# A tiled 8192 x 8192 transpose: the first load issued as two halves from two engines, and the last wait moved to VectorE

## Chip, cores and metric

The kernel runs on one core of a Trainium2 chip. The metric is the time of one execution on the device, in microseconds. A profile of one execution lies beside the times. In it PE is TensorE, DVE is VectorE, ACT is ScalarE, POOL is GpSimd and SP is SyncE.

## What is computed

```python
x = np.random.randn(8192, 8192).astype(np.float32)

def reference(x):
    return np.transpose(x)
```

The matrix has 8192 x 8192 float32 elements, 268 MB. It is read once and its transpose is written once.

## The kernel before

The input is cut into 128 chunks of 128 rows by 4096 columns (2 MB each): `chunks` at line 99 runs over two column halves `s` and, within each, over 64 row blocks `c`. A chunk is loaded whole into one of three buffers, `in0` to `in2`, each with 128 partitions of 16 KB (`NIN` is 3, so chunk `t` goes to buffer `t % 3`).

TensorE transposes a chunk in 32 blocks of 128 x 128 against an identity matrix into PSUM (`transposes`, lines 112 to 123). Its program is a loop, `turns`, of three chunks a turn. ScalarE copies the first half of a chunk's blocks from PSUM to SBUF, VectorE the second half (line 241). The copies go into nine regions of one SBUF tensor, `regs`. Each region gathers the columns of up to eight chunks (`W` is 8), so that a store can write long runs; the eight windows are offset by one chunk against each other, so that about one of them closes per chunk. A region that is complete is stored by one DMA (line 174 the first, line 28 the rest) from ScalarE's queue. In the first eight chunks the closing windows are still short, and the stores grow from 256 KB to 2 MB; the last chunk closes all eight, and these eight stores stand at the end.

The order of the work around the change:

- GpSimd builds the identity matrix (lines 85 to 94).
- The loads of the first three chunks are issued from SyncE (`load`, line 103), one behind the other on its queue. In the code these three calls stand behind TensorE's loop. Every later load is issued from ScalarE, and stands in its program behind the copies and stores of the chunk that freed the buffer (lines 261 to 264).
- Each input buffer has one semaphore, `s_ld[k]`. TensorE starts on a chunk when it reaches 18 and takes 18 off (line 113): 16 come from the load's DMA, 1 each from ScalarE and VectorE, which increment it when they have copied the chunk that was there before and thereby free PSUM. For the very first chunk there is nothing to copy before, so lines 96 and 97 give the two increments at once.
- Each region has a semaphore `s_st[r]`, raised by 16 for each of its stores. At the end SyncE waits for all nine regions (lines 265 and 266), so that the kernel ends only when every store has landed. `free` is the list of regions in the order in which their stores were issued; its last entry is the region that was stored last.

Of the kernel before, what the change touches and what calls it, by code (L numbers as in the profile page):

```python
# [40 lines left out]
def kernel(  # L41
# [13 lines left out]
    nc = tc.nc  # L55
    P = 128
# [8 lines left out]
    NIN = 3  # L65
    NREG = 9
    CH = N // P
    J = S * P

    with tc.tile_critical():  # L70
        nc.alloc_sbuf_tensor("pad", [P, 32], dt)
        ident = nc.alloc_sbuf_tensor("ident", [P, P], dt).ap()
        ins = [nc.alloc_sbuf_tensor(f"in{k}", [P, J], dt).ap() for k in range(NIN)]
# [6 lines left out]
        s_ld = [nc.alloc_semaphore(f"s_ld{k}") for k in range(NIN)]  # L80
        s_st = [nc.alloc_semaphore(f"s_st{k}") for k in range(NREG)]
# [6 lines left out]
            out=ident,  # L88
            in_=ident,
# [3 lines left out]
            pattern=[[-1, P]],  # L93
            channel_multiplier=1,
        ).then_inc(s_id, 1)
        nc.vector.sem_inc(s_ld[0], 1)
        nc.scalar.sem_inc(s_ld[0], 1)

        chunks = [(s, c) for s in range(M // J) for c in range(CH)]

        def load(t):
            s, c = chunks[t]
            (nc.sync if t < NIN else nc.scalar).dma_start(
                out=ins[t % NIN], in_=x[c * P:(c + 1) * P, s * J:(s + 1) * J]
            ).then_inc(s_ld[t % NIN], 16)

        def transposes(k):
            nc.tensor.sem_inc(s_ld[k], -18).wait_op(s_ld[k], 18, "sem-ge")  # L113
            for q in range(NR):
                e, g = divmod(q, NH)
                for b in range(B):
                    tr = nc.tensor.transpose(  # L117
                        pss[e][:, (g * B + b) * P:(g * B + b + 1) * P],
                        ins[k][:, q * B * P + b:(q + 1) * B * P - B + b + 1:B],
                        ident,  # L120
                    )
                if q % 2:
                    tr.then_inc(s_pe, 1)
# [15 lines left out]
            nc.regs_alu(turn, turn, 1, op=mybir.AluOpType.add)  # L139
            nc.tensor.br_lt(turn, T // NIN + 1, on_true="turns", on_false="done")  # L140
        nc.switch_bb("done")

        for t in range(NIN):
            load(t)

        copied = [0, 0]
        free = list(range(NREG))
        stored = [0] * NREG
# [36 lines left out]
        for t, (s, c) in enumerate(chunks):  # L185
            closed = []
            for e in range(2):
# [5 lines left out]
                for q in range(e * NH, (e + 1) * NH):  # L193
                    if q not in window:
# [4 lines left out]
                        r = free.pop(0)  # L199
# [6 lines left out]
                    t0, r, parts = window[q]  # L206
# [54 lines left out]
            if t + NIN < T:  # L261
                if not closed:
                    nc.scalar.wait_ge(s_pe, (t + 1) * NH)
                load(t + NIN)
        for r in range(NREG):
            nc.sync.wait_ge(s_st[r], 16 * stored[r])


# [28 lines left out]
```

## Time and profile before

| | |
|---|---|
| time, median of 3 runs | 1261.94 us (1261.61 to 1261.95) |
| span of the profiled execution | 1260.4 us |
| TensorE matmul, busy | 739.0 us |
| VectorE, busy | 302.0 us |
| ScalarE, busy | 253.5 us |
| moved by DMA | 536.95 MB, mean 426 GB/s |
| DMA packets on SyncE's queue (q1) and ScalarE's (q10) | 432 and 38832 |

The span is the time from the first to the last instruction of the profiled execution; that execution is known by its span alone, and the times of the runs are longer than it by some 1.5 us. In a row of a timeline stand the start, the time taken, the engine ("SPq" and "ACTq" are the instruction queues of SyncE and ScalarE, where a DMA is issued), the line, the operation, and in brackets the idle time before it with what ended it. A row of a table by stretches holds the stretch, its length, the busy time of PE, of its weight loads, of DVE, ACT and POOL with the number of instructions, the granted TensorE clock, the busy share of the 16 DMA engines and their GB/s; a packet is booked where it starts, so that neighbouring short stretches can differ by more than the stream does. In a row of one source line stand the operation's count, its least, median and greatest duration in ns, and the starts of the first and the last.

### The profile page before, as it was taken

The page shows a single profiled execution, that of the slowest core. Times are in us where ns is not written, and L with a number is a line of the kernel's source. Part 1 is how long each engine was busy: PE and PEld are TensorE (multiplying, and loading weights), DVE is VectorE, ACT ScalarE, POOL GpSimd, SP SyncE. Part 2 cuts the span into 40 slices and gives each one's busy share as a digit, 9 for nine tenths or more (in the row PEclk, how much of TensorE's full clock was granted, in tenths as well). Part 3 has the DMA queues.
Part 4 walks back from the last instruction along what each step waited for, and adds up shares of the span by engine and source line. Part 5 has one row for each costly group of instructions (what it writes and reads, how often), then busy time and mean ns, then how long its engine had stood idle before and what let it go on. Part 6 is the DMA issues. An engine that isn't in the chain of part 4 may idle for free. (4 is left out here: it accounts for less than half of the span.)

```text
span 1260.4 us, 9367 instructions
## 1 busy us (share of the span) xinstructions
PE 739.0 (59%) x4096; PEld 718.4 (57%) x4096; DVE 302.0 (24%) x250; ACT 253.5 (20%) x257; POOL 0.7 (0%) x6
## 2 busy tenths in 40 slices
PE   5656556565566655565556656566565655665561
PEld 5556556565556655565555656565565655665561
DVE  2322222222222222222222222222222222222220
ACT  3212211122111211122111211121111211121110
POOL 0000000000000000000000000000000000000000
PEclk9886876868777777778687786867777687777776
DMA  9999999999999999999999999999999999999998
GB/s 383 429 422 426 425 430 431 426 431 431 427 430 431 428 428 431 428 429 432 427 422 426 429 429 425 431 429 428 430 428 428 431 428 429 429 429 429 429 431 376
DMA packets 39271, 536.95 MB, mean 426 GB/s; under 512 B 4320, under 2 KB 4832, under 8 KB 6240
## 3 DMA queue, kind: packets, MB, share of 16 engines
q10 hardware_dynamic: 38832, 530.60, 99.0%
q1 hardware_dynamic: 432, 6.29, 1.2%
q14 instruction: 6, 0.05, 0.0%
q8 instruction: 1, 0.02, 0.0%
HBM read 268.44 MB, written 268.44 MB: 426 GB/s over the span
## 5 line engine op out<-in xcount | busy, mean ns | idle before, releaser
L117 PE MATMUL ps<-ident,in 128*128 128x128 f32 x4096 | 739.0, 362 | 493.5 <-PEq L113 493.5
L117 PEld LDWEIGHTS ps<-ident,in 128*128 128x128 f32 x4096 | 718.4, 220 | 513.9 <-issue 513.9
L241 DVE COPY regs<-ps 128x512 f32<-128x512 f32 (+3 forms) x250 | 302.0, 1246 | 932.1 <-PE ps L117 932.1
L241 ACT COPY regs<-ps 128x512 f32<-128x512 f32 (+3 forms) x256 | 252.2, 1016 | 978.8 <-PE ps L117 760.8
L241 ACT ACT_TABLE_LOAD x1 | 1.3, 1283 | 1.0 <-SPq L70 1.0
L87 POOL TENSOR_SCALAR_AFFINE_SELECT ident<-ident 128x128 f32<-128x128 f32 x1 | 0.3, 293 | 0.2 <-POOL ident L85 0.2
L85 POOL MEMSET ident<- 128x128 f32 x1 | 0.2, 204 | 0.5 <-SPq L70 0.5
L281 POOL MEMSET const-bfloat16-1.0<- 128x1 bf16 x1 | 0.1, 102 | 0.0
L281 POOL MEMSET const-uint8-127<- 128x1 uint8 x1 | 0.1, 102 | 0.0
L281 POOL MEMSET const-float32-0.0<- 128x1 f32 x1 | 0.1, 99 | 0.2 <-issue 0.2
L281 POOL MEMSET const-float32-1.0<- 128x1 f32 x1 | 0.1, 99 | 0.0
## 6 DMA issues: line engine op xcount, KB each, us to landing
in<-in_x_dram ACTq DMA_DIRECT2D x125, 2048.0 KB, 16.8
out_dram<-regs ACTq DMA_DIRECT2D x114, 2048.0 KB, 12.6
out_dram<-regs ACTq DMA_DIRECT2D x4, 1792.0 KB, 11.1
in<-in_x_dram SPq DMA_DIRECT2D x3, 2048.0 KB, 11.7
out_dram<-regs ACTq DMA_DIRECT2D x4, 1536.0 KB, 12.5
out_dram<-regs ACTq DMA_DIRECT2D x4, 1280.0 KB, 11.5
out_dram<-regs ACTq DMA_DIRECT2D x4, 1024.0 KB, 11.1
out_dram<-regs ACTq DMA_DIRECT2D x4, 768.0 KB, 12.3
```

The lines of the kernel that those rows point to most:

```text
L85: nc.gpsimd.memset(ident, 0.0).then_inc(s_id, 1)
L87: nc.gpsimd.affine_select(out=ident, in_=ident, compare_op=mybir.AluOpType.not_equal, fill=1.0, base=0, pattern=[[-1, P]], channel_multipl ...
L117: tr = nc.tensor.transpose(pss[e][:, (g * B + b) * P:(g * B + b + 1) * P], ins[k][:, q * B * P + b:(q + 1) * B * P - B + b + 1:B], ident,)
L241: cp = nc.scalar.copy(out=o, in_=i) if e == 0 else nc.vector.tensor_copy(out=o, in_=i)
L281: nc = _bacc.Bacc("TRN2", target_bir_lowering=False, num_devices=1)
```

## The change

The first chunk's load becomes two DMAs. ScalarE issues partitions 0 to 63, SyncE partitions 64 to 127, both as the first DMA of their queue. ScalarE's half raises `s_ld[0]` by 16; SyncE's half raises a new semaphore, `s_l0`. ScalarE adds its 1 right after the issue. VectorE waits for `s_l0` and then adds its 1, so that the 18 are complete only when both halves are in. The three first loads now stand ahead of TensorE's loop in the code. At the end VectorE waits for the region that was stored last, and SyncE for the other eight.

```diff
-        nc.vector.sem_inc(s_ld[0], 1)
-        nc.scalar.sem_inc(s_ld[0], 1)
+        s_l0 = nc.alloc_semaphore("s_l0")
...
         def load(t):
             s, c = chunks[t]
-            (nc.sync if t < NIN else nc.scalar).dma_start(
-                out=ins[t % NIN], in_=x[c * P:(c + 1) * P, s * J:(s + 1) * J]
-            ).then_inc(s_ld[t % NIN], 16)
+            src = x[c * P:(c + 1) * P, s * J:(s + 1) * J]
+            if t == 0:
+                nc.scalar.dma_start(out=ins[t][:P // 2], in_=src[:P // 2]).then_inc(s_ld[t], 16)
+                nc.sync.dma_start(out=ins[t][P // 2:], in_=src[P // 2:]).then_inc(s_l0, 16)
+                nc.scalar.sem_inc(s_ld[t], 1)
+                nc.vector.wait_ge(s_l0, 16)
+                nc.vector.sem_inc(s_ld[t], 1)
+                return
+            (nc.sync if t < NIN else nc.scalar).dma_start(out=ins[t % NIN], in_=src).then_inc(s_ld[t % NIN], 16)
+
+        for t in range(NIN):
+            load(t)
...
         nc.switch_bb("done")
-
-        for t in range(NIN):
-            load(t)
...
         for r in range(NREG):
-            nc.sync.wait_ge(s_st[r], 16 * stored[r])
+            (nc.vector if r == free[-1] else nc.sync).wait_ge(s_st[r], 16 * stored[r])
```

## The prediction

> **What bounds the kernel now.** I read the page's head and DMA rows first, then the engines' busy shares and issue rows, then a table by stretches.
>
> ```profile
> span 1260.4 us, 9367 instructions
> PE 739.0 (59%) x4096; PEld 718.4 (57%) x4096; DVE 302.0 (24%) x250; ACT 253.5 (20%) x257; POOL 0.7 (0%) x6
> ...
> DMA  9999999999999999999999999999999999999998
> ...
> DMA packets 39271, 536.95 MB, mean 426 GB/s; under 512 B 4320, under 2 KB 4832, under 8 KB 6240
> q10 hardware_dynamic: 38832, 530.60, 99.0%
> q1 hardware_dynamic: 432, 6.29, 1.2%
> HBM read 268.44 MB, written 268.44 MB: 426 GB/s over the span
> ```
>
> No compute engine is busy for more than 59% of the span, while the 16 DMA engines are busy in every slice. Queue q10 (ScalarE's, 530.60 MB) carries nearly everything; q1 (SyncE's) carries 6.29 MB, the first three loads of 2.1 MB each. So the kernel is a stream of 536.95 MB, and its end is start of stream + bytes over rate + what follows the last byte. The table by stretches shows these pieces:
>
> ```profile
> 2.00:4.00 2.00, 0.00 (x0) 0.00 (x0) 0.00 (x0) 0.26 (x1) 0.00 (x0) 1.00 0.91 303
> 4.00:14.00 10.00, 5.50 (x32) 5.34 (x32) 1.03 (x2) 2.15 (x4) 0.00 (x0) 1.00 1.02 436
> 14.00:24.00 10.00, 6.70 (x53) 6.57 (x54) 3.94 (x7) 3.49 (x7) 0.00 (x0) 1.00 0.99 386
> 100.00:1230.00 1130.00, 677.45 (x3694) 658.94 (x3695) 271.14 (x214) 225.69 (x222) 0.00 (x0) 0.75 1.01 429
> ```
>
> The last two columns are the DMA engines' busy share and GB/s. The stream runs saturated: 436 GB/s over 4 to 14 us, when the first loads are alone in it, and 429 GB/s in the long middle. There is no idle DMA time between, so **a microsecond lost to the stream anywhere comes out at the end, and a microsecond won by another engine does not**, as long as the stream always has something queued. The chain of waits names PE and VectorE near the end, but VectorE's last copies end at 1234, and the rest is the drain of stores:
>
> ```profile
> 1231.57 2.48 DVE L241 COPY regs<-ps 128x512 f32<-128x512 f32 x4 [7.54 <-PE ps L117]
> ```
>
> **The start, and the cover in it.**
>
> ```profile
> 0.94 1.32 SPq L103 DMA_DIRECT2D in<-in_x_dram  x3
> 0.94 0.20 POOL L85 MEMSET ident<- 128x128 f32 x1 [0.50 <-SPq L70]
> 0.98 1.28 ACT L241 ACT_TABLE_LOAD   x1 [0.98 <-SPq L70]
> ...
> 8.40 5.50 PE L117 MATMUL ps<-ident,in 128*128 128x128 f32 x32 [8.40 <-PEq L113]
> ...
> 11.01 0.63 ACTq L174 DMA_DIRECT2D out_dram<-regs  x1
> ...
> 12.97 2.48 DVE L241 COPY regs<-ps 128x512 f32<-128x512 f32 x4 [12.97 <-PE ps L117]
> 13.94 0.36 ACTq L103 DMA_DIRECT2D in<-in_x_dram  x1
> ```
>
> ```profile
> 1.50:2.00 0.50, 0.00 (x0) 0.00 (x0) 0.00 (x0) 0.50 (x1) 0.17 (x1) 1.00 0.00 0
> 2.00:2.25 0.25, 0.00 (x0) 0.00 (x0) 0.00 (x0) 0.25 (x1) 0.00 (x0) 1.00 1.67 328
> ```
>
> ```profile
> 2.00:3.00 1.00, 0.00 (x0) 0.00 (x0) 0.00 (x0) 0.26 (x1) 0.00 (x0) 1.00 1.01 262
> ```
>
> ```profile
> L103 ACTq DMA_DIRECT2D in<-in_x_dram x125: 334/607/1218, 13.9 to 1210.1; - x125
> L103 SPq DMA_DIRECT2D in<-in_x_dram x3: 372/423/427, 0.9 to 1.8; - x3
> ...
> DMA to landing us min/median/max: 7.3/16.8/19.8
> ```
>
> The first data moves between 2.00 and 2.25. The first load is issued at 0.94 and lands 7.3 us later, at 8.2; PE begins at 8.4. Each further load takes 2.097 MB / 436 GB/s = 4.81 us, so the three are in at about 8.2 + 2 x 4.81 = 17.9. The fourth load is issued at 13.94, and its data can begin about 1.1 us after (the first issue at 0.94 gives data from about 2.0), at 15.0. Hence PE may begin up to 17.9 - 15.0 = **2.9 us later** before the stream runs dry. That is why an earlier PE start is worth nothing here.
>
> **The change part by part.**
>
> 1. *Loads written ahead of the PE loop.* SyncE's first issue stands at 0.94, the same moment as GpSimd's memset that already stood ahead of that loop. Both follow the same release. Nothing to win: 0.
>
> 2. *Two issues instead of one.* ScalarE issues its 64 rows where its semaphore increment stood (about 0.9), SyncE its 64 rows at 0.94, then loads 1 and 2. An issue of 128 rows costs SyncE 372 to 427 ns. If half the rows cost half, data may start up to 0.2 us earlier; if not, nothing is won. I take -0.1. ScalarE pays one more issue (334 to 1218 ns by its own rows) and its 1.28 us table load moves behind it or stays ahead of it. Its next work is the copy at 10.4, so at most 2.5 us lie beside about 8 us of waiting. If the table load stays ahead, ScalarE's half starts 1.28 us late; PE would then be late by that, inside the cover of 2.9 us.
>
> 3. *How fast two halves travel.* This is the term that decides. No row of this trace shows a load of 64 rows; all have 128 rows, and there 436 GB/s belongs to 16 DMA engines and 128 partitions at once. If the rate belongs to the engines, two halves on two queues move as the whole did, 4.81 us: cost 0, or slightly below with item 2. If it belongs to the partitions being written (3.4 GB/s a row), a half alone goes at 218 GB/s. Then it matters whether all engines work on the same half at a time. A 16 KB row of a load takes an engine 16384 B / (436/16 GB/s) = 0.60 us, and the stretch of 2 to 3 us moved 262 KB, which is 16 such rows: all engines start within less than two rows' time. Engines that start so close together and take rows from two queues in turn all serve the same half for much of the time, and stay so, since the turns are equally long. Fully in step, the first 2.1 MB take 9.62 us instead of 4.81: **+4.81** is the upper end. The nearest row with two queues in the stream is 14 to 24 us (the first store, issued at 11.01, beside the third load, which ends near 18): 386 GB/s at a busy share of 0.99, against 436 at 1.02. Engines just as busy moved 11% less, which on the first load would be 4.81 x 436/386 - 4.81 = +0.6; but small store pieces are in that row, so it prices only a mild case. I take three quarters of the upper end, **+3.6**, because engines partly out of step lose less, and because the slowest engine, not the average, sets when a load has landed and when the stream ends. Both ends, 0 and +4.8, are kept for the range.
>
>    [...]
>
>    The loss is not hidden: PE starts at about 12 instead of 8.4 and the fourth load is issued 3.6 us later, but the first three loads end 3.6 us later too, so the cover of 2.9 us stays as it was, nothing runs dry, and the whole later stream is shifted by 3.6.
>
> 4. *VectorE waits for SyncE's half and then increments.* Queued behind that wait are only its increment and its first copy, at 12.97, which waits for PE anyway. PE waits for the increment: one more semaphore hop, about 0.1 us by the distance between the first landing (8.2) and PE's wait and start (8.3, 8.4). It lies in the 2.9 us cover: 0. Without cover, 0.1.
>
> 5. *The last wait on VectorE.*
>
> ```profile
> L266 SPq EVENT_SEMAPHORE  x4: 27/28/4912, 1250.4 to 1254.3; - x4
> ```
>
> ```profile
> L70 SPq EVENT_SEMAPHORE  x3: 17/28/28, 1259.4 to 1259.6; - x3
> L70 SPq NOP  x2: 13/13/13, 0.7 to 1259.7; - x2
> L70 SPq COMPARE_BRANCH  x1: 33/33/33, 1259.2 to 1259.2; - x1
> ...
> L70 DVEq DRAIN  x1: 17/17/17, 1259.4 to 1259.4; - x1
> ```
>
>    SyncE's last wait starts at 1254.3 and lasts 4.9 us, to 1259.2. Then come its branch (1259.2), its signal (1259.4), the other engines' drains (1259.4), and the closing barrier to 1260.4. If VectorE waits instead, SyncE's signal and three of the drains are done early, and only VectorE's wake, branch and drain follow the last landing. VectorE was done with its copies at 1234, so nothing is queued behind it. At best that saves the step from the wait's end to the signal, 0.2 us; at worst VectorE's branch and drain take as long, 0. I take -0.1.
>
> Sum: 1260.4 + 0 - 0.1 + 3.6 + 0 - 0.1 = 1263.8. The span before is 1260.4, the median of the three times 1261.94, so 1.5 us lie around the span: **1265.3 us**, +3.4 or 0.27%.
>
> **The rivals.**
>
> - *The halves run at full rate (the other side: not slower).* The rate belongs to the engines, or the two halves keep out of step so that all 128 partitions are served at once. For it: in every long row the busy share is about 1.0 whatever mix of loads and stores runs, so the engines look like the limit. Against it: such a row never has fewer than 128 partitions in any one transfer. Then only items 2 and 5 count: 1261.94 - 0.2 = 1261.7, and between 1261.3 and 1262.0. The point from which it decides: the first load lands by 8.5 or earlier.
> - *Partly in step.* Some engine pairs collide, others don't, or the loss is of the kind in the 14-to-24 row: +0.6 to +2.4, so about 1263.3.
> - *The stream runs dry.* ScalarE's half comes late (table load ahead, a slow issue up to 1.2 us): 1.28 + 1.2 = 2.5 us of delay to PE against 2.9 us of cover. At full rate it costs nothing; it would decide only above 2.9 us. I count it within the first rival.
> - *Clearly faster.* It would need 2.5 us, and ahead of the stream lie about 2 us and behind the last landing 1.2, of which this change touches 0.4. Only a luckier interleaving of the later stream could give it (the rows of 429 and 436 GB/s differ by 1.6%, so some of that exists).
>
> **Chances.** Halves mostly in step, 1264.3 to 1266.7, forecast 1265.3: 0.55. Partly in step: 0.10. Full rate: 0.33. Clearly faster: 0.02. The mildness of the only two-queue row speaks against more than 0.55; that every loss in the head is paid in full, while all gains together stay below 0.4 us, speaks against less. About 0.2%, 2.5 us, is what a measurement of this kernel can tell from no change. Slower by more than that (above 1264.5) is nearly all of the first case, 0.55; within it are the second and third, 0.43; faster is 0.02. The range is 1261.3 to 1266.8: from the best of the full-rate case to the in-step case at its upper end. The forecast's own range is 1264.3 to 1266.7.
>
> **What would show it.** Right: in the profile after, the rate between 3 and 10 us falls toward 220 to 300 GB/s at a busy share near 1.0; PE's first matmul stands near 12 instead of 8.4; later rows keep 429 GB/s; the fourth load is issued near 17.6. Wrong: PE starts at 8.5 or earlier and the early rate is 430 or so (full rate), or PE starts near 12 and the time is still below 1262.5 (the shift was absorbed, and the stream had slack that I do not see). Item 5 is right if SyncE's signal stands near 1254 relative to the old end and the stretch from last landing to end is 1.1 us rather than 1.2. A middle rate other than 429 GB/s would mean that something I left out moved the time.

## The result

The changed kernel takes 1268.51 us (median of 6 runs, 1266.66 to 1272.21) against 1261.78 us (6 runs, 1261.39 to 1261.97): a ratio of 1.0055, 95% interval 1.0043 to 1.0066, so +6.7 us by the medians. The direction was forecast, the size (+3.4 us) was too small, and the time lies above the stated range. The profiled execution is the shortest of the six, 1266.66 us with a span of 1264.9 us.

The table by stretches of the changed kernel (last columns: granted clock, busy share of the DMA engines, GB/s):

```profile
2.00:4.00 2.00, 0.00 (x0) 0.00 (x0) 0.00 (x0) 0.90 (x1) 0.00 (x0) 1.00 1.08 254
4.00:14.00 10.00, 0.00 (x0) 0.00 (x0) 0.00 (x0) 0.00 (x0) 0.00 (x0) 1.00 0.97 221
14.00:24.00 10.00, 6.53 (x37) 6.40 (x38) 2.48 (x4) 2.15 (x4) 0.00 (x0) 1.00 1.01 410
24.00:40.00 16.00, 11.71 (x93) 11.20 (x92) 6.79 (x12) 6.39 (x11) 0.00 (x0) 1.00 1.00 418
40.00:100.00 60.00, 36.79 (x230) 35.70 (x231) 17.28 (x18) 14.19 (x14) 0.00 (x0) 0.82 1.01 422
100.00:1230.00 1130.00, 682.63 (x3708) 663.88 (x3706) 273.12 (x214) 227.25 (x223) 0.00 (x0) 0.74 1.01 429
```

The two stretches of the kernel before that the prediction did not show:

```profile
24.00:40.00 16.00, 10.89 (x87) 10.41 (x87) 7.46 (x12) 4.92 (x7) 0.00 (x0) 1.00 1.02 431
40.00:100.00 60.00, 35.99 (x217) 34.83 (x215) 15.92 (x13) 14.17 (x14) 0.00 (x0) 0.83 1.01 425
```

From 4 to 14 us the engines are as busy as before (0.97 against 1.02), but they move 221 GB/s instead of 436. By 24 us the stream has moved 2 x 254 + 10 x 221 + 10 x 410 = 6.82 MB instead of 2 x 303 + 10 x 436 + 10 x 386 = 8.83 MB; at 429 GB/s that is 4.7 us behind. From 24 to 100 us it falls back by another 0.39 MB, 0.9 us. After that the rates are equal to the digit shown. The span grew by 4.5 us, 1.1 us less than these two add up to; that lies within the rounding, since 1 GB/s over 1130 us would be 2.6 us.

The head of the timeline:

```profile
0.91 0.61 ACTq L104 DMA_DIRECT2D in<-in_x_dram  x1
0.94 0.20 POOL L85 MEMSET ident<- 128x128 f32 x1 [0.50 <-SPq L70]
0.95 0.56 SPq L105 DMA_DIRECT2D in<-in_x_dram  x1
...
1.56 1.04 SPq L110 DMA_DIRECT2D in<-in_x_dram  x2
1.62 1.28 ACT L246 ACT_TABLE_LOAD   x1 [1.62 <-SPq L70]
...
15.76 5.91 PE L125 MATMUL ps<-ident,in 128*128 128x128 f32 x32 [15.76 <-PEq L121]
...
21.70 0.36 ACTq L110 DMA_DIRECT2D in<-in_x_dram  x1
```

Both halves are issued at once, at 0.91 and 0.95, and the table load moved behind ScalarE's issue. Yet TensorE starts at 15.76 instead of 8.40. From issue to landing, line 104 (ScalarE's half) and line 105 (SyncE's half) say why:

```profile
DMA to landing us min/median/max: 14.7/14.7/14.7
```

```profile
DMA to landing us min/median/max: 8.8/8.8/8.8
```

SyncE's half is in at 9.7, ScalarE's at 15.6. The DMA queues from 2 to 6.5 us, then from 6.5 to 14 us, show the order (packets, MB, share of 16 engines; a packet is one row of 16 KB, but the last 54 hold 0.62 MB, which is 38 rows, so 16 of them carry none):

```profile
q1 hardware_dynamic: 64, 1.05, 107.0%
```

```profile
q10 hardware_dynamic: 64, 1.05, 59.0%
q1 hardware_dynamic: 54, 0.62, 35.5%
```

All 64 rows of SyncE's half (q1) start before the first row of ScalarE's (q10). So the halves do not travel side by side: one goes, at about half rate (233 GB/s from 2 to 6.5 us), and then the other, in turns with the rows of the second load (223 GB/s from 6.5 to 14 us).

### The profile page after: what moved, and what is told of

It reads as the page before. It is cut to its first block, busy times and chain, and to the rows that moved or that the text cites. A ratio compares the mean times of both kernels' runs of the same rounds, so it can differ in the third digit from the quotient of the medians.

```text
span 1264.9 us, 9369 instructions
## 1 busy us (share of the span) xinstructions
PE 743.2 (59%) x4096; PEld 722.6 (57%) x4096; DVE 302.2 (24%) x250; ACT 253.6 (20%) x257; POOL 0.7 (0%) x6
```

## The experiments

Each is the changed kernel with one edit, unless it says otherwise. Where a diff shows `+` lines alone for the first load, they stand in place of the two `dma_start` lines of the change. Times are medians; the ratio to the kernel before, run on the same chip, follows with its interval. There the kernel before had medians of 1261.82, 1261.93 and 1262.74 us in the three groups, with single runs up to 1267.9, so one run alone says little.

**The changed kernel again.**

> The changed kernel once more, beside the next three, to have its loss on the same chip and a second profile. If what it lost in its first profile (first data of ScalarE's half at about 6.8, rows of both queues slow until about 14.4, first matmul at 15.8) is a fixed property, the early stretch repeats and the time is +4.5 to +8 us; if the longer runs among its first six (up to 1272.2) come from the head of the stream, the early stretch differs from profile to profile.

1269.24 us (6 runs, 1267.84 to 1274.0), ratio 1.0059 (1.0043 to 1.0076). Its profiled execution was a long one, 1271.88 us with a span of 1270.1:

```profile
4.00:14.00 10.00, 0.00 (x0) 0.00 (x0) 0.00 (x0) 0.00 (x0) 0.00 (x0) 1.00 1.00 213
14.00:24.00 10.00, 5.91 (x32) 5.75 (x32) 1.43 (x3) 2.15 (x4) 0.00 (x0) 1.00 0.97 372
24.00:40.00 16.00, 11.39 (x90) 11.10 (x91) 6.04 (x11) 5.86 (x11) 0.00 (x0) 1.00 1.00 383
40.00:100.00 60.00, 35.28 (x232) 33.96 (x230) 18.99 (x20) 14.70 (x16) 0.00 (x0) 0.86 1.01 418
```

The slow head repeats, and here it lasts longer: line 104's landing takes 16.6 us instead of 14.7. The stretch from 24 to 100 us is slower too, by 1.19 MB or 2.8 us against the kernel before. By 100 us the stream is 8.6 us behind, nearly all of the 9.7 us by which this span is longer: this long run lost its time in the head and shortly after it. That need not hold for every long run: that of the column halves below had its head at the full rate (438 GB/s from 4 to 14 us) and was slower in the long middle (427 GB/s from 100 to 1230 us, against 429).

**The last wait alone** (the kernel before, with this edit):

```diff
-            nc.sync.wait_ge(s_st[r], 16 * stored[r])
+            (nc.vector if r == free[-1] else nc.sync).wait_ge(s_st[r], 16 * stored[r])
```

> The kernel before with item 5 alone: VectorE waits for the region stored last, the loads are as they were. My prediction took -0.1 us for it (0 to -0.2), so a span of 1260.3 and a first matmul at 8.4 as before. If the loss of the changed kernel came from its end (a wait that is slow to wake, or a closing barrier that grows), this kernel would be about 4 us or more slower. If all of it comes from the first load, it is within 0.3 us of the kernel before.

1262.2 us (12 runs), ratio 0.9996 (0.9985 to 1.0007), first matmul at 8.33, 436 GB/s from 4 to 14 us. The last wait costs and wins nothing that can be measured. The loss lies in the loads; their new place in the code costs nothing either, as the column halves below show.

**Both halves on one queue.**

```diff
-                nc.scalar.dma_start(out=ins[t][:P // 2], in_=src[:P // 2]).then_inc(s_ld[t], 16)
+                nc.sync.dma_start(out=ins[t][:P // 2], in_=src[:P // 2]).then_inc(s_ld[t], 16)
```

> The changed kernel, but both halves are issued by SyncE, one behind the other, so no two queues are in the stream while the first three loads run. Theory P (the rate belongs to the partitions written, 64 rows go at half rate): both halves go at about 205 to 220 GB/s, one after the other, the first load lands near 2.3 + 10 = 12.5, loads two and three then run at 430 GB/s; PE starts near 12.7 and the time is +4.5 to +5 us. Rival Q (two queues in turns are what is slow): the stream runs at 430 GB/s from the start, PE starts near 8.5, time within 0.3 us of before.

1266.25 us (11 runs, 1265.76 to 1267.34), ratio 1.003 (1.0021 to 1.0039), +4.4 us. The stream and the start of TensorE (this timeline ends at 18 us, so the row counts 25 of the chunk's 32 matmuls):

```profile
4.00:14.00 10.00, 0.28 (x2) 0.31 (x3) 0.00 (x0) 0.00 (x0) 0.00 (x0) 1.00 0.97 231
14.00:24.00 10.00, 8.29 (x58) 8.13 (x58) 2.48 (x4) 3.42 (x7) 0.00 (x0) 1.00 1.02 426
```

```profile
13.72 4.55 PE L125 MATMUL ps<-ident,in 128*128 128x128 f32 x25 [13.72 <-PEq L121]
```

With no second queue in the head the two halves are still slow, so rival Q (two queues in turns are what is slow) falls as the main cause. What the change loses beyond this, 2 to 3 us, does not appear without the second queue.

**Which side of the transfer.** In the next two kernels only the rows read, or only the partitions written, differ from the change; the first chunk's output columns stand in another order.

```diff
-                nc.scalar.dma_start(out=ins[t][:P // 2], in_=src[:P // 2]).then_inc(s_ld[t], 16)
-                nc.sync.dma_start(out=ins[t][P // 2:], in_=src[P // 2:]).then_inc(s_l0, 16)
+                nc.scalar.dma_start(out=ins[t][:P // 2], in_=src[0::2]).then_inc(s_ld[t], 16)
+                nc.sync.dma_start(out=ins[t][P // 2:], in_=src[1::2]).then_inc(s_l0, 16)
```

> The changed kernel, but ScalarE's half reads the even rows of the block into partitions 0 to 63 and SyncE's half the odd rows into partitions 64 to 127, so the first chunk's output columns stand in another order. The partitions written are those of the change, only the source rows differ. Theory P (a contiguous half of the partitions is written at half rate): as slow as the change, early rate 200 to 260 GB/s, +4 to +8 us. Theory H (it is the neighbouring source rows): early rate above 400 GB/s, within 1.5 us of before.

1268.02 us (4 runs), ratio 1.0051 (1.0036 to 1.0065).

```diff
+                nc.scalar.dma_start(out=ins[t][0::2], in_=src[:P // 2]).then_inc(s_ld[t], 16)
+                nc.sync.dma_start(out=ins[t][1::2], in_=src[P // 2:]).then_inc(s_l0, 16)
```

> The changed kernel, but ScalarE's half (rows 0 to 63 of the block) goes to the even partitions and SyncE's half (rows 64 to 127) to the odd ones, so the first chunk's output columns stand in another order. The rows read are those of the change, only the partitions written differ. [...] Theory H (64 neighbouring source rows are slow to read from memory): early rate 200 to 260 GB/s as in the change and +4 to +10 us.

1263.38 us (12 runs), ratio 1.0009 (0.9998 to 1.0021). The stretch from 4 to 14 us, first with alternate source rows, then with alternate partitions:

```profile
4.00:14.00 10.00, 0.00 (x0) 0.00 (x0) 0.00 (x0) 0.00 (x0) 0.00 (x0) 1.00 0.99 231
```

```profile
4.00:14.00 10.00, 3.24 (x16) 3.27 (x17) 0.00 (x0) 0.59 (x1) 0.00 (x0) 1.00 1.01 429
```

Other source rows change nothing; other partitions bring the full rate back, with the same 64 rows on the same two queues. Theory P (it is the partitions written) holds, theory H (it is the neighbouring source rows) falls. Here too SyncE's half lands first (6.0 us after its issue, ScalarE's after 9.7) and TensorE starts at 10.76, 2.4 us late. At the full rate that lies inside the cover of 2.9 us, the delay of TensorE that the prediction allowed before the stream runs dry, and the time cannot be told from that of the kernel before.

**Which 64 partitions.** All on SyncE:

```diff
+                nc.sync.dma_start(out=ins[t][32:96], in_=src[32:96]).then_inc(s_ld[t], 16)
+                nc.sync.dma_start(out=ins[t][:32], in_=src[:32]).then_inc(s_l0, 16)
+                nc.sync.dma_start(out=ins[t][96:], in_=src[96:]).then_inc(s_l0, 16)
...
-                nc.vector.wait_ge(s_l0, 16)
+                nc.vector.wait_ge(s_l0, 32)
```

> The one-queue experiment with other cuts: SyncE issues partitions 32 to 95 first, then 0 to 31, then 96 to 127. Theory W (64 neighbouring partitions are slow as such, whichever they are): the first 64 rows again run at 200 to 220 GB/s from 2.3 to about 7.4. Theory M (what counts is which ways into SBUF the partitions reach): the first 64 rows run at 400 GB/s or more and are in by about 5, the two quarters after them at about half rate, so the first load is in near 10 to 10.5, PE starts near 10.5 and the time is +1.7 to +2.6 us. [...]

1264.26 us (10 runs), ratio 1.001 (0.9998 to 1.0021), +1.5 us by the medians. While partitions 32 to 95 come in (two stretches, since one microsecond alone says little), and while the outer two quarters do:

```profile
3.00:5.00 2.00, 0.00 (x0) 0.00 (x0) 0.00 (x0) 0.00 (x0) 0.00 (x0) 1.00 0.86 360
4.00:5.00 1.00, 0.00 (x0) 0.00 (x0) 0.00 (x0) 0.00 (x0) 0.00 (x0) 1.00 1.04 442
```

```profile
6.00:10.00 4.00, 0.00 (x0) 0.00 (x0) 0.00 (x0) 0.00 (x0) 0.00 (x0) 1.00 1.01 221
```

From 3 to 5 us the changed kernel moved 238 GB/s and the kernel before 393. Sixty-four neighbouring partitions run at or near the full rate when they are 32 to 95, and 0 to 31 and 96 to 127 run at half rate: theory W falls, and the rates are near those that theory M expected. TensorE starts at 11.85, not near 10.5 as expected.

What the runs show goes by the partitions written: a transfer within 0 to 63 or within 64 to 127 ran at about half rate (221 and 231 GB/s for the halves, 221 for the quarters), and one with as many partitions from the one as from the other at or near the full rate (429 for every second partition, 360 to 442 for 32 to 95). The ways into SBUF that theory M speaks of are a supposition; no run shows them.

**Halves by columns.**

```diff
+                nc.scalar.dma_start(out=ins[t][:, :J // 2], in_=src[:, :J // 2]).then_inc(s_ld[t], 16)
+                nc.sync.dma_start(out=ins[t][:, J // 2:], in_=src[:, J // 2:]).then_inc(s_l0, 16)
```

> The changed kernel, but the first load is halved by columns: 128 partitions by 2048 columns (8 KB a row) each, one half from ScalarE, one from SyncE, side by side as in the change. Theory P: every transfer has 128 partitions, so the stream runs at 420 GB/s or more from the start; the ScalarE half may come late and PE starts between 8.5 and 13, but the stream loses nothing and the time is within 0.6 us of before. Rival Q: the early rate is 200 to 260 GB/s while ScalarE's half is under way, and the time is +4 us or more.

1262.11 us (12 runs), ratio 0.9999 (0.999 to 1.0008); the profiled execution was the longest of them, 1266.91, and only its head is used here. The stream, and the queues from 2 to 7.5 us:

```profile
4.00:14.00 10.00, 5.43 (x31) 5.46 (x32) 0.57 (x1) 2.15 (x4) 0.00 (x0) 1.00 1.03 438
```

```profile
q1 hardware_dynamic: 127, 1.04, 53.1%
q10 hardware_dynamic: 125, 1.01, 44.3%
```

These halves do travel side by side, row about row, at the full rate. TensorE starts at 8.57 (8.40 before), so issuing the load twice did not bring it in sooner.

**Two loads cut.** The one-queue kernel, with the second load cut in the same way:

```diff
+        s_l1 = nc.alloc_semaphore("s_l1")
...
+            if t == 1:
+                nc.sync.dma_start(out=ins[t][:P // 2], in_=src[:P // 2]).then_inc(s_l1, 16)
+                nc.sync.dma_start(out=ins[t][P // 2:], in_=src[P // 2:]).then_inc(s_l1, 16)
+                return
...
+        nc.sync.wait_ge(s_l1, 32)
+        nc.sync.sem_inc(s_ld[1], 16)
```

> The one-queue experiment with the second load cut into two halves of 64 partitions as well, all on SyncE. If each load cut so costs a full 4.4 to 4.9 us of stream and nothing absorbs it, the time is +8.8 to +9.8 us, and the early rate stays at 200 to 230 GB/s until about 22 us. If part of the loss is absorbed later (the stream had slack), the second cut costs clearly less than the first, and the time is below +7.5 us.

1271.4 us (4 runs), ratio 1.0077 (1.0063 to 1.0092), +9.5 us: twice the loss of one. The stream has no slack that absorbs it.

```profile
4.00:14.00 10.00, 0.19 (x1) 0.22 (x2) 0.00 (x0) 0.00 (x0) 0.00 (x0) 1.00 1.01 215
14.00:22.00 8.00, 5.25 (x32) 5.06 (x31) 2.48 (x4) 2.15 (x4) 0.00 (x0) 1.00 0.99 207
```

**The second load held back.**

```diff
         for t in range(NIN):
+            if t == 1:
+                nc.sync.wait_ge(s_l0, 16)
             load(t)
```

> The changed kernel, but SyncE issues the second load only when its own half has landed, so that ScalarE's half does not take turns with the second load's rows. Theory S (what the change loses beyond two half-rate halves, about 2 us, comes from ScalarE's late half taking turns with full-width rows, which are then slow too): the slow stretch ends near 12.5 instead of 14.4, PE starts near 13, and the time is that of the one-queue experiment, +4 to +4.8 us. Rival: the extra loss comes from something else in the change and stays, +5.5 us or more.

1266.64 us (5 runs, 1266.11 to 1269.16), ratio 1.0039 (1.0026 to 1.0052), beside 1269.24 for the change on the same chip. ScalarE's half now lands 12.8 us after its issue instead of 14.7 and 16.6, TensorE starts at 13.87, and the stretches after it are no longer below those of the kernel before:

```profile
14.00:24.00 10.00, 8.29 (x53) 8.13 (x54) 2.48 (x4) 3.22 (x6) 0.00 (x0) 1.00 1.03 429
24.00:40.00 16.00, 10.88 (x86) 10.40 (x86) 7.45 (x12) 5.31 (x9) 0.00 (x0) 1.00 1.02 431
```

This is what theory S (the further loss comes from ScalarE's late half taking turns with the second load) expected: the time is that of the one-queue kernel within 0.4 us. The intervals of this ratio and of the change's overlap; four of the five runs are below all six of the change. The bytes say the same. From 2 to 100 us the kernel before moved 41.19 MB, the one-queue kernel 39.45, this one 39.37, the change 38.85 in its first profile and 37.50 in its second. At 429 GB/s that is 4.1, 4.2, 5.5 and 8.6 us behind.

**The first load whole, on ScalarE's queue.**

```diff
-                nc.scalar.dma_start(out=ins[t][:P // 2], in_=src[:P // 2]).then_inc(s_ld[t], 16)
-                nc.sync.dma_start(out=ins[t][P // 2:], in_=src[P // 2:]).then_inc(s_l0, 16)
+                nc.scalar.dma_start(out=ins[t], in_=src).then_inc(s_ld[t], 16)
...
-                nc.vector.wait_ge(s_l0, 16)
```

> The first load whole on ScalarE's queue, loads two and three on SyncE's, so that two queues share the stream from the start but no transfer has fewer than 128 partitions. If two queues in turns cost the stream nothing by themselves, the early rate is 420 GB/s or more; the first load shares with the second and lands between 9 and 13, PE starts that late, and since the cover before the stream runs dry is about 3 us the time is within 0.8 us of before up to a start of 11.3, and +0 to +2 us beyond. If ScalarE's queue only begins after the rows that SyncE's queue already handed over, its first data stand 1 to 4 us after SyncE's.

1266.55 us (10 runs), ratio 1.0026 (1.0013 to 1.004). Two whole loads in turns run at full rate, so two queues by themselves cost the stream nothing here, but then comes what the rival "the stream runs dry" described:

```profile
4.00:16.00 12.00, 2.61 (x13) 2.64 (x14) 0.00 (x0) 0.59 (x1) 0.00 (x0) 1.00 1.01 431
16.00:20.00 4.00, 3.58 (x21) 3.39 (x20) 1.34 (x3) 1.57 (x3) 0.00 (x0) 1.00 0.45 164
```

```profile
13.39 6.19 PE L123 MATMUL ps<-ident,in 128*128 128x128 f32 x32 [13.39 <-PEq L119]
16.00 0.63 ACTq L177 DMA_DIRECT2D out_dram<-regs  x1
19.61 0.34 ACTq L108 DMA_DIRECT2D in<-in_x_dram  x1
```

TensorE starts 5.0 us late and the fourth load is issued at 19.61, after the three loads are in (near 17.9, the estimate for the kernel before): from 16 to 20 us the busy share is 0.45. So a cover exists: 2.4 us with alternate partitions cost nothing that can be told, 5.0 us here ran the stream dry. The price, +3.8 us, is above the +0 to +2 us expected. The profiled execution was the longest of its runs (1271.39), but its head accounts for the median: by the bytes moved, the stream is 2.5 us behind at 24 us, 3.7 at 40 and 4.1 at 100. So the dry stretch cost 2.5 us and the stream behind it 1.6 more; why the latter is slow stays open. What this one execution lost besides, it lost later: 427 GB/s from 100 to 1230 us, against 429.

## Why the prediction came out as it did

*What bounds the kernel: right.* The stream has no slack. One load at half rate costs 4.4 us, two cost 9.5, and the last wait nothing. Of the signs named, the early rate (221 GB/s) and the kept middle rate (429) came as forecast; TensorE (15.76, not near 12) and the fourth load (21.70, not near 17.6) came later.

*Item 1, order in the code: right*, SyncE's first issue stays at 0.95.

*Item 2, the issue: wrong in sign, small.* Half the rows do not cost half an issue: 557 ns on SyncE and 606 on ScalarE for 64 rows, against 372 to 427 for 128 in the kernel before. No data move from 2.00 to 2.25, where the kernel before had begun:

```profile
2.00:2.25 0.25, 0.00 (x0) 0.00 (x0) 0.00 (x0) 0.25 (x1) 0.00 (x0) 1.00 0.00 0
```

*Item 3, how fast two halves travel: the mechanism right, the picture and the size wrong.* This is the step that failed: the term taken as +3.6 us measured +6.7. "If it belongs to the partitions being written" was the right branch, and the experiments on sides and partitions settle it. But I had both halves taking turns from the start, with engine pairs out of step losing less, and so took three quarters of +4.81. There was no such discount. SyncE's half went alone, all engines on the same 64 partitions (its 64 rows took 107% of the 16 engines' time from 2 to 6.5 us), and then ScalarE's: the one-queue kernel, in which the halves go one after the other, loses 4.4 us. And +4.81 was no upper end. ScalarE's late half then took turns with the second load, and meanwhile those full-width rows were slow as well. From 9 to 10 us every row that started was one of the second load's, 15 in all, and together they took 108% of the 16 engines' time in that microsecond: 1.15 us a row, against the prediction's 0.60. From 12 to 14 us the changed kernel was still near half rate, while the one-queue kernel was leaving it:

```profile
12.00:14.00 2.00, 0.00 (x0) 0.00 (x0) 0.00 (x0) 0.00 (x0) 0.00 (x0) 1.00 0.96 246
```

```profile
12.00:14.00 2.00, 0.28 (x2) 0.31 (x3) 0.00 (x0) 0.00 (x0) 0.00 (x0) 1.00 0.94 336
```

As far as these runs show, that makes the further 2 to 3 us, beside the 4.4: by 100 us the change's two profiles are 5.5 and 8.6 us behind, the held-back load 4.2. The first of these profiles is of the change's shortest run, with a span (1264.9) no longer than that of the held-back load (1265.0); the further loss stands in the medians and in the second profile.

*The cover: right that the stream does not run dry, wrong that the cover stays as it was.* The reason given held, the first three loads ended later too: SyncE's queue still started rows after 22 us (0.26 MB from 22 to 24 us), where in the kernel before none started after 18. But TensorE was 7.4 us late, and the fourth load was issued at 21.70 instead of 13.94, so that the cover of 2.9 us was all but used up. No dry stretch shows (410 GB/s from 14 to 24 us at a busy share of 1.01). The whole first load on ScalarE's queue shows what comes beyond it.

*Item 4, VectorE's wait: right.* SyncE's half, for which it waits, landed at 9.7, and TensorE waited for ScalarE's until 15.6.

*Item 5, the end: right in kind, and not worth 0.1 us.* SyncE now signals early and waits for VectorE:

```profile
L70 SPq EVENT_SEMAPHORE  x3: 17/28/28, 1259.1 to 1264.0; - x3
...
L70 DVEq COMPARE_BRANCH  x1: 47/47/47, 1263.7 to 1263.7; - x1
L70 DVEq DRAIN  x1: 17/17/17, 1263.9 to 1263.9; - x1
```

From VectorE's branch at 1263.7 to the end at 1264.9 it is 1.2 us, as it was from SyncE's.

*The 1.5 us around the span: a little small.* In the runs here of which time and span are both known, they differ by 1.7 to 1.9 us.

No version here beats the kernel before. The best are the column halves (0.999 to 1.0008) and the last wait alone (0.9985 to 1.0007), which are equal to it.

What stays open: why ScalarE's half of 64 rows, issued first, began only after all of SyncE's, while the column halves alternated from the start; and why the full-width rows of the second load were slow between rows of the late half. Both were seen, neither was taken apart. Open too is why the change's times spread from 1266.66 to 1274.0.

## What to carry to other kernels

When a kernel is bound by its DMA stream, read from the stretch table what a change does to the rate while the busy share stays at 1.0: here a start of TensorE 2.4 us later cost nothing that could be told, and slow bytes were paid in full. Cut a load by columns (438 GB/s from 4 to 14 us here), or so that each part takes as many partitions from 0 to 63 as from 64 to 127 (429 with every second partition), not into those two halves (221). Before trusting that two queues run side by side, look at the packets of each queue in the first microseconds.

## What was not expected of the hardware

- Issuing 64 rows of 16 KB took 557 to 606 ns, 128 rows 372 to 427 ns on SyncE in the kernel before (432 to 564 behind the half in the changed one).
- Partitions 32 to 95 took a load at 360 GB/s over two microseconds and 442 in the second of them, while 0 to 31 and 96 to 127 took theirs at 221 with the engines at a busy share of 1.01.
- Of two halves issued 0.04 us apart from two queues, all rows of one started before the other's first row; as column halves they alternated (127 and 125 packets by 7.5 us).
